# The low part of split weights made by a negated copy on ScalarE and an accumulating DMA, in place of a subtraction

## The chip, the cores and the metric

One core of a Trainium2 chip runs the whole kernel. The metric is the device time of one execution in microseconds (us). The kernel before was run three times: 1477.27, 1478.51 and 1480.23 us, so the median is 1478.51 us.

The engines are named as in the profile: PE is TensorE (matmuls), DVE is VectorE, ACT is ScalarE, POOL is GpSimd, SP is SyncE. SP does nothing here but issue DMAs; POOL and ACT issue some too.

## The reference, cut to what matters

Two layers of a sequence model over 512 tokens of 1024 features, batch 1, float32. Each layer has a projection of the normalised input, two kinds of mixers, an output projection, and a feed-forward part:

```
h = rms_norm(x, norm_mix[l]);  u = h @ w_in
layer 0: y = [hgrn2_mix(...), rwkv7_mix(...)] @ w_out
layer 1: y = [s5_mix(...), mlstm_mix(...)] @ w_out
x = x + y
h = rms_norm(x, norm_ffn[l])
x = x + (silu(h @ w_gate) * (h @ w_up)) @ w_down      # hidden size 2816
...
out = rms_norm(x, norm_final)
```

All that the change touches is how the weight matrices (`w_in`, `w_out`, `w_gate`, `w_up`, `w_down`) reach TensorE.

## The kernel before

Activations are kept transposed: features on the 128 partitions, the 512 tokens in the free dimension. A dense product is made of 128x128 blocks of weights against 128x512 blocks of activations. To keep float32 accuracy with the rounded type float32r, each operand is split into two parts, w = hi + lo and a = hh + hl, and every block takes three matmuls (`mm3`): hi with hh, hi with hl, lo with hh, in this order.

The weights are read from DRAM as **units**, listed in `order` in the order of their use. A full unit is 128x1024 (512 KB, eight blocks, 24 matmuls); the units of the output projections have 640 or 768 columns, and every third unit of a down projection (`wD`) has 768. `wget` hands out a unit and first calls `wissue` for the unit after it (AHEAD = 1). `wissue` does three things:

- SP loads the unit into one of two buffers `raw`.
- ACT copies it, 256 columns at a time, into float32r tiles `hi` (L369, in `split`). This rounds.
- DVE subtracts, lo = raw - hi, also 256 columns at a time (L370); for nine units of layer 0 (the list `pu`) POOL does it.

The pool `whl` has eight `hi` and eight `lo` tiles of 256 columns, which is two units of each. A tile is written again when the last matmul that reads its old content has ended, so the first quarter of a unit can be remade when a quarter of the unit two places before it has been used. Two narrow units (`wL`, `wG`) hold both parts side by side, and the last unit of the program is split into the tiles of the normalised input, which are free by then.

Each engine works through its own queue in order. The order in a queue is made when the program is built, by a scheduler that goes by the program's own order and by estimated costs; the names of tiles that it waits for are turned into semaphores.

Around this machinery the program has these stretches: layer 0's projections woven with the HGRN2 and RWKV-7 mixers (the RWKV-7 part inverts small triangular blocks on POOL, `rw_inverse`, and moves them by DMAs that POOL issues); the output projection (`wO0a`, `wO0b`); feed-forward part 0 (44 units `wGU0`, gate and up in turn, then 24 units `wD0`); layer 1's projections woven with S5 (POOL, with some twenty DMAs of its own) and mLSTM; the output projection (`wO1a`, `wO1b`); feed-forward part 1. In the feed-forward part (`ffn`) DVE takes a gate product out of PSUM (L1184), ACT applies Silu (L247), DVE multiplies the up product in (L1187, L1188), and ACT and DVE split the result into `ah` and `al`.

Of the kernel before, what the change touches and what calls it, by code (L numbers as in the profile page):

```python
# [11 lines left out]
F32R = mybir.dt.float32r  # L12
U32 = mybir.dt.uint32
AF = mybir.ActivationFunctionType
# [72 lines left out]
def _cols(w, cols):  # L87
    """[K, N] -> [len(cols)/128, 128, K]: per column tile, k tiles side by side."""
    a = w[:, cols]
    k, n = a.shape  # L90
    a = a.reshape(k // P, P, n // P, P)
    return np.ascontiguousarray(a.transpose(2, 1, 0, 3).reshape(n // P, P, k))


def _rows(w, cols, per):
    """[K, N] -> [K/(128 per), 128, per N]: per k tiles side by side, all columns."""
    a = w[:, cols]
    k, n = a.shape
    a = a.reshape(k // (P * per), per, P, n)
    return np.ascontiguousarray(a.transpose(0, 2, 1, 3).reshape(k // (P * per), P, per * n))  # L100


def _layout(i):
# [78 lines left out]
    # S5: partitions hold (group of the pair, state), free dims the pair of groups  # L182
# [20 lines left out]
def trunk(ctx: ExitStack, tc: tile.TileContext, A, out, dbg=None, start=0):  # L203
# [8 lines left out]
    class Pools:  # L212
        """pools that are opened one by one and closed together"""
# [25 lines left out]
    def act(o, i, f, bias=0.0, scale=1.0):  # L239
        """one table load for all the activations of a set that follow each other"""  # L240
        want = SETS.get(f)
        if want is not None and want != epoch["set"]:
            ld = S.preload_act_table_set(want)
            for u in epoch["users"]:
                tc.add_manual_dep(ld.ins, u, NOSYNC, reason="table")
            epoch.update(set=want, load=ld.ins.name, users=[])
        a = S.activation(o, i, f, bias=bias, scale=scale)  # L247
        if want is not None:
            tc.add_manual_dep(a.ins, epoch["load"], NOSYNC, reason="table")
            epoch["users"].append(a.ins.name)  # L250

    def sigmoid(o, x, nbias=0.0):
        """1 / (1 + exp(-x - bias)) by exp and ln alone"""
        act(o, x, AF.Exp, bias=nbias, scale=-1.0)
        act(o, o, AF.Ln, bias=1.0)
        act(o, o, AF.Exp, scale=-1.0)

    def newton(r_, v, t):
        """one step towards r_ = v ** -0.5"""
        act(t, r_, AF.Square)  # L260
        V.scalar_tensor_tensor(t, v, -0.5, t, MUL, MUL)  # L261
        V.scalar_tensor_tensor(r_, t, 1.5, r_, ADD, MUL)  # L262
# [14 lines left out]
    def ts(op, i, j, o, a, scale, bias, bias_s=None):  # L277
        """o = a * scale + bias"""
        e = on(op, i, j)
        if e is S:  # L280
            act(o, a, AF.Identity, bias=bias if bias_s is None else bias_s, scale=scale)
        else:
            e.tensor_scalar(o, a, scale, bias, MUL, ADD)
# [17 lines left out]
    # the weights in the order of their use, loaded and split ahead of it  # L301
# [20 lines left out]
    def onpool(unit, part):  # L322
        return unit in PRM["pu"] and part in PRM["c"]
# [7 lines left out]
    def wissue():  # L331
        nm, u, c0, n = order[pos[1]]
        raw = whl.tile([P, 1024], F32, tag="raw", name="raw", bufs=2)
        nc.sync.dma_start(raw[:, :n], A[nm][u][:, c0:c0 + n])
        parts = []
        last = nm == "wD1" and u == KD - 1
        if last and c0 == 0:
            wlast.extend(htiles()[:2])
        if nm in NARROW:
            # both parts of few columns, side by side  # L340
            m = NARROW[nm]
            for c in range(0, n, WP // 2):
                w = whl.tile([P, WP], F32R, tag=("hi", "lo")[len(parts) * m * 2 // WP % 2], name="w")
                w4 = w.rearrange("p (k s c) -> p k s c", s=2, c=m)
                split(w4[:, :, 0, :], w4[:, :, 1, :], raw[:, c:c + WP // 2].rearrange("p (k c) -> p k c", c=m))
                parts += [w[:, j:j + 2 * m] for j in range(0, WP, 2 * m)]
            n = 0
        for c in range(0, n, WP):
            m = min(n - c, WP)
            if last:  # L350
                hi, lo = (t.rearrange("p k t -> p (k t)")[:, c0 + c:c0 + c + m] for t in wlast)
            else:
                hi = whl.tile([P, WP], F32R, tag="hi", name="hi")
                lo = whl.tile([P, WP], F32R, tag="lo", name="lo")
            split(hi[:, :m], lo[:, :m], raw[:, c:c + m], G if onpool(pos[1], c // WP) else V)
            parts += [(hi[:, j:j + P], lo[:, j:j + P]) for j in range(0, m, P)]
        ready.append(parts)
        pos[1] += 1
# [8 lines left out]
    def split(h, l, src, eng=V):  # L367
        """src (SBUF, float32) = h + l"""
        S.copy(h, src)  # L369
        eng.tensor_tensor(l, src, h.bitcast(F32), SUB)  # L370
# [9 lines left out]
    def defer(f):  # L380
        """f after the next dense product; more banks until its result is there"""
        later.append(f)
        early[0] = PRM.get("d", 2)
# [27 lines left out]
    def run(gen, until=None):  # L411
        """advance a stream to its mark (or its end); its result"""
        while True:
            try:
                if next(gen) == until and until is not None:
                    return None
            except StopIteration as e:
                return e.value
# [4 lines left out]
    def weave(*streams):  # L423
        """emit streams side by side, each up to its mark, in proportion to the costs that they yield"""
        live = [[0.0, j, g, m] for j, (g, m) in enumerate(streams)]
        while live:
            e = min(live, key=lambda t: t[:2])
            v = next(e[2], None)
            if v is None or v == e[3]:
                live.remove(e)  # L430
            elif not isinstance(v, str):
                e[0] += v
# [5 lines left out]
    def beside(*gens):  # L438
        """streams side by side as one stream"""
# [10 lines left out]
    class Norm:  # L450
        """hh + hl = x * gain, tile by tile; rstd = 1 / rms of x on all partitions"""
# [72 lines left out]
    # ================= S5: discretised parameters, kept in DRAM until layer 1 =================  # L524
    def s5_setup(p5):
# [54 lines left out]
        # (lambda_bar - 1) / lambda  # L580
# [65 lines left out]
    # ================= layer 0: HGRN2 and RWKV-7 =================  # L646
    def layer0():
# [20 lines left out]
        # lower bounds: softmax over the table's rows, first row  # L668
# [14 lines left out]
        # 1 - ka, 1 - mu  # L683
# [27 lines left out]
        def hgrn(h):  # L711
# [30 lines left out]
            # attention inside the chunks: pairs of tokens, then blocks about their midpoints  # L742
# [9 lines left out]
            for l, n in enumerate((1, 32, 16, 8, 4, 2)):  # L752
                pp = mtile()
                if n > 1:
# [9 lines left out]
                    # only the columns of the later halves  # L764
# [12 lines left out]
            # states between the chunks  # L777
# [35 lines left out]
            # head norm, gain, gate  # L813
# [23 lines left out]
        # block-diagonal tiles: the zeros are written once  # L837
# [48 lines left out]
        def rw_prep(g, p):  # L886
# [7 lines left out]
            # decays up to a token (er) and up to the one before it (ea)  # L894
# [8 lines left out]
            # normalised key  # L903
# [18 lines left out]
            # bonus  # L922
# [4 lines left out]
            # products of the chunks  # L927
# [18 lines left out]
            # token-major forms  # L946
# [23 lines left out]
        def rw_inverse(q, g):  # L970
            """inverse of I - A on the diagonal blocks of 32 tokens, in place, a block per partition"""
# [48 lines left out]
        def rw_chain(g, p):  # L1020
            """states (values by keys) and outputs, chunk after chunk"""
# [25 lines left out]
            # norm over each head, bonus, gate  # L1047
# [128 lines left out]
    # ================= output projection, feed-forward =================  # L1176
    def ffn(l, x, hh, hl, rstd, pf, on_ready, side=()):
# [15 lines left out]
        for n in range(KD):  # L1193
            ps = dtile()
            if l == 1 and n == KD - 1:
                # half of the tokens after the other: the end of one beside the products of the next
# [67 lines left out]
    # ================= layer 1: S5 and mLSTM =================  # L1264
# [207 lines left out]
    AGI = {}  # L1472

    def gates():
# [6 lines left out]
        # log sigmoid  # L1481
# [12 lines left out]
        # sums over blocks of 128 tokens, running maximum  # L1494
# [25 lines left out]
        # rows of the heads to the partitions in ROW  # L1520
# [159 lines left out]
    # ================= final norm =================  # L1680
# [56 lines left out]
```

## Time and profile before

| | |
|---|---|
| median of three runs | 1478.51 us |
| span of the profiled execution | 1480.0 us |
| matmul records / weight loads | 6668 / 6668 |
| DVE, POOL subtractions of full tiles (128x256) at L370 | 759 x 462 ns, 34 x 882 ns |
| ACT casts 128x256 at L369 | 793 x 404 ns |
| DRAM traffic | 121.71 MB read, 10.39 MB written |

The page shows one execution on the chip. Busy times are per engine; a matmul's record is longer than its share of PE's time, since matmuls overlap in the array, so the rate is read from the starts of neighbouring matmuls. "PEclk" is the clock that TensorE was granted, 1.00 for full. In lists of waits, "A <- B" says that B ended A's wait.

### The profile page before, as it was taken

The numbers are of one execution on the slowest core, as the hardware profiler recorded it, in microseconds if no ns is written. First come the engines' busy times: TensorE is split into PE (matmuls) and PEld (weight loads), VectorE is DVE, ScalarE is ACT, GpSimd is POOL, SyncE is SP. The second block draws the span as 40 slices with busy tenths as digits, with TensorE's granted clock in tenths as the row PEclk, the third lists the DMA queues.
The fourth block names the chain that finished last, engine by engine and source line by source line (L and its number), as shares of the span: only waits on it lengthen the run. The fifth ranks groups of instructions, "written<-read, shape, count | busy, mean of one in ns | idle before, by whom it ended". The sixth has DMA issues, their size and how long they took to land. (4 is left out here: it accounts for less than half of the span.)

```text
span 1480.0 us, 19897 instructions
## 1 busy us (share of the span) xinstructions
PE 1423.6 (96%) x6668; PEld 1140.6 (77%) x6668; DVE 965.1 (65%) x2035; ACT 681.2 (46%) x1594; POOL 356.2 (24%) x538
## 2 busy tenths in 40 slices
PE   8989999988999999999999899999999999999996
PEld 5777878767787888888888678766778888888885
DVE  7589669899688555555444677679785555554333
ACT  7554565645465333333333333477464343333332
POOL 5367740678320333110010542100020000000001
PEclk9989989998999999999999999999999999999998
DMA  5211221021323333333343832311233323323331
GB/s 186 86 36 46 63 71 50 30 56 47 116 84 100 108 102 102 106 97 105 104 128 100 208 107 80 113 57 29 64 102 92 100 89 97 100 86 96 91 109 62
DMA packets 51142, 133.39 MB, mean 90 GB/s; under 512 B 10640, under 2 KB 16272, under 8 KB 50784
## 3 DMA queue, kind: packets, MB, share of 16 engines
q1 hardware_dynamic: 38656, 116.86, 25.9%
q0 software_dynamic: 3024, 7.26, 2.0%
q10 hardware_dynamic: 9360, 8.00, 1.8%
q8 instruction: 53, 0.87, 0.2%
q14 instruction: 49, 0.40, 0.1%
HBM read 121.71 MB, written 10.39 MB: 89 GB/s over the span
## 5 line engine op out<-in xcount | busy, mean ns | idle before, releaser
L369 ACT CAST hi<-raw 128x256 fp32r<-128x256 f32 (+1 forms) x809 | 317.9, 402 | 528.7 <-PE d L286 480.1
L370 DVE TENSOR_TENSOR lo<-raw,hi 128x256 fp32r<-128x256 f32 (+1 forms) x774 | 348.0, 459 | 295.3 <-ACT hi L369 281.1
L286 PE MATMUL d<-hh,hi 128*128 128x512 f32 x1088 | 443.3, 407 | 2.9 <-DVE ur L1077 2.9
L286 PE MATMUL d<-hl,hi 128*128 128x512 f32 x1088 | 438.9, 403 | 0.0
L286 PE MATMUL d<-hh,lo 128*128 128x512 f32 x1088 | 438.9, 403 | 0.0
L286 PEld LDWEIGHTS d<-hh,hi 128*128 128x128 f32 x1088 | 208.4, 192 | 52.7 <-DVE ur L1077 3.4
L286 PEld LDWEIGHTS d<-hh,lo 128*128 128x128 f32 x1088 | 208.2, 191 | 49.0 <-issue 1.1
L286 PEld LDWEIGHTS d<-hl,hi 128*128 128x128 f32 x1088 | 208.2, 191 | 48.7 <-issue 2.4
L286 PE MATMUL d<-ah,hi 128*128 128x512 f32 x330 | 129.4, 392 | 0.0
L286 PE MATMUL d<-ah,lo 128*128 128x512 f32 x330 | 129.4, 392 | 0.0
L286 PE MATMUL d<-al,hi 128*128 128x512 f32 x330 | 129.4, 392 | 0.0
L1706 POOL TENSOR_TENSOR x<-x,f 128x256 f32<-128x256 f32 x6 | 5.2, 890 | 368.7 <-issue 362.2
L286 PE MATMUL d<-ysp,hi 128*128 128x512 f32 x224 | 74.1, 407 | 2.6 <-DVE x L1164 0.9
L467 POOL TENSOR_TENSOR rstd<-rstd,sq 128x512 f32<-128x512 f32 x21 | 28.6, 1363 | 193.9 <-ACT sq L247 183.7
L980 POOL TENSOR_TENSOR iu<-iu,ti 32x30 f32<-32x30 f32 (+14 forms) x120 | 71.3, 594 | 9.2
L286 PEld LDWEIGHTS d<-ah,hi 128*128 128x128 f32 x330 | 61.9, 188 | 14.0
L286 PEld LDWEIGHTS d<-al,hi 128*128 128x128 f32 x330 | 61.9, 188 | 13.9
L286 PEld LDWEIGHTS d<-ah,lo 128*128 128x128 f32 x330 | 61.9, 188 | 13.8
L978 POOL TENSOR_TENSOR ti<-iu 32x30 f32<-32x30 f32 (+14 forms) x120 | 70.3, 586 | 9.0
L286 PEld LDWEIGHTS d<-ysp,hi 128*128 128x128 f32 x224 | 41.2, 189 | 12.9 <-issue 1.9
L1187 DVE TENSOR_TENSOR g<-d,g 128x512 f32<-128x512 f32 x42 | 29.0, 691 | 27.5 <-PE d L286 27.5
L286 PE MATMUL d<-ysp,lo 128*128 128x512 f32 x112 | 45.5, 406 | 0.7 <-DVE lo L370 0.7
(489 smaller groups left out, 2046.1 us busy)
## 6 DMA issues: line engine op xcount, KB each, us to landing
raw<-in_wGU_dram SPq DMA_DIRECT2D x88, 512.0 KB, 3.6
raw<-in_wD_dram SPq DMA_DIRECT2D x32, 512.0 KB, 3.6
raw<-in_wA_dram SPq DMA_DIRECT2D x16, 512.0 KB, 3.6
raw<-in_wB_dram SPq DMA_DIRECT2D x13, 512.0 KB, 3.7
raw<-in_wD_dram SPq DMA_DIRECT2D x16, 384.0 KB, 3.1
raw<-in_wV_dram SPq DMA_DIRECT2D x6, 512.0 KB, 5.3
raw<-in_wQ_dram SPq DMA_DIRECT2D x6, 512.0 KB, 3.7
raw<-in_wK_dram SPq DMA_DIRECT2D x6, 512.0 KB, 3.6
```

The lines of the kernel that those rows point to most:

```text
L286: T.matmul(o, w, a, start=start, stop=stop)
L369: S.copy(h, src)
L370: eng.tensor_tensor(l, src, h.bitcast(F32), SUB)
L467: self.eng.tensor_tensor(self.rstd, self.rstd, sq, ADD)
L978: G.tensor_tensor(t3, iu[:, j:j + 1, j + 1:].to_broadcast([32, j, n]), iu[:, 0:j, j:j + 1].to_broadcast([32, j, n]), MUL)
L980: G.tensor_tensor(iu[:, 0:j, j + 1:], iu[:, 0:j, j + 1:], t3, ADD)
L1187: V.tensor_tensor(g1, pu_, g1, MUL)
L1706: G.tensor_tensor(x[k][:, t], x[k][:, t], r_, MUL)
```

## The change

`wissue` is rewritten for all units but the first, the two narrow ones and the last of the program (three entries of `order`). For the 211 others:

- ACT makes `hi` in pieces of 512 columns, with four buffers (two units, as before).
- ACT also makes lo = -raw, rounded to float32r, in pieces of 512, into a tile `lo` of 1024 columns, with two buffers. Since rounding is symmetric, this is -hi.
- POOL then issues one DMA for the whole unit, which reads the weights from DRAM a second time and adds them to `lo` (`accum_op=ADD`). The sum is raw - hi.

The subtractions on DVE and POOL go. `raw` keeps its two buffers, SP's load is as before.

```
-        nc.sync.dma_start(raw[:, :n], A[nm][u][:, c0:c0 + n])
+        src = A[nm][u][:, c0:c0 + n]
+        nc.sync.dma_start(raw[:, :n], src)
...
-        for c in range(0, n, WP):
-            m = min(n - c, WP)
-            if last:
...
-            else:
-                hi = whl.tile([P, WP], F32R, tag="hi", name="hi")
-                lo = whl.tile([P, WP], F32R, tag="lo", name="lo")
-            split(hi[:, :m], lo[:, :m], raw[:, c:c + m], G if onpool(pos[1], c // WP) else V)
-            parts += [(hi[:, j:j + P], lo[:, j:j + P]) for j in range(0, m, P)]
...
+        else:
+            direct = pos[1] < PRM.get("direct", 1)
+            lo = whl.tile([P, 1024], F32R, tag="lo", name="lo", bufs=2)
+            for c in range(0, n, 512):
+                m = min(n - c, 512)
+                hi = whl.tile([P, 512], F32R, tag="hi", name="hi", bufs=4)
+                if direct:
+                    for e in range(0, m, 256):
+                        f = min(m, e + 256)
+                        split(hi[:, e:f], lo[:, c + e:c + f], raw[:, c + e:c + f])
+                else:
+                    S.copy(hi[:, :m], raw[:, c:c + m])
+                    S.activation(lo[:, c:c + m], raw[:, c:c + m], AF.Copy, scale=-1.0)
+                parts += [(hi[:, j:j + P], lo[:, c + j:c + j + P]) for j in range(0, m, P)]
+            if not direct:
+                G.dma_start(lo[:, :n], src, accum_op=ADD)
```

The rest of the diff takes comments out, so line numbers differ by 14 behind `wissue`: L286 stays, L369 and L370 of `split` become L383 and L384, and the new lines are L366 (hi), L367 (negated copy) and L370 (the DMA).

**ACT's queue in feed-forward part 0.** `hi_6708` and so on are 256-column pieces of one unit, `g1` is a gate tile on which Silu works, `ah18` a split result. Before:

```order
L369 CAST hi_6708<-raw_6706 128x256 [waits DMAHW6_49,PE_49,Activation_49]
L369 CAST hi_6712<-raw_6706 128x256 [waits PE_49,Activation_49]
L369 CAST hi_6716<-raw_6706 128x256 [waits PE_49,Activation_49]
L369 CAST hi_6720<-raw_6706 128x256 [waits PE_49,Activation_49]
L369 CAST hi_6754<-raw_6752 128x256 [waits DMAHW7_49,PE_49,Activation_49]
L369 CAST ah18_6687<-g1_6639 128x512 [waits DVE_49]
```

The same place now, for one gate unit (`lo_6154`) and the row behind it:

```order
L366 CAST hi_6155<-raw_6152 128x512 [waits DMAHW7_49,PE_49,Activation_49]
L366 CAST hi_6158<-raw_6152 128x512 [waits PE_49,Activation_49]
L367 ACTIVATE lo_6154<-raw_6152 128x512 [waits DMASW6_49,PE_49,Activation_49]
L247 ACTIVATE g1_6149<-g1_6149 128x512 [waits DVE_49]
L367 ACTIVATE lo_6154<-raw_6152 128x512
L366 CAST hi_6210<-raw_6207 128x512 [waits DMAHW0_49,PE_49,Activation_49]
```

Each quarter of `hi` waited for PE on its own; now the first half of `lo` waits for PE once for its whole buffer, and a Silu stands between the two halves in every second unit.

**PE's queue at a unit's start in the same part.** `d` is the PSUM tile, `hh` and `hl` the two parts of the activations. Before, two blocks of a unit (the third row has no wait, since DVE's subtraction is covered by the wait ahead of it):

```order
L286 MATMUL d_6770<-hh_4449,hi_6708 128x512 [waits DVE_49,Activation_49]
L286 MATMUL d_6770<-hl_4450,hi_6708 128x512
L286 MATMUL d_6770<-hh_4449,lo_6709 128x512
L286 MATMUL d_6770<-hh_4449,hi_6708 128x512
L286 MATMUL d_6770<-hl_4450,hi_6708 128x512
L286 MATMUL d_6770<-hh_4449,lo_6709 128x512
```

Now:

```order
L286 MATMUL d_6124<-hh_4181,hi_6061 128x512 [waits DVE_49,Activation_49]
L286 MATMUL d_6124<-hl_4182,hi_6061 128x512
L286 MATMUL d_6124<-hh_4181,lo_6060 128x512 [waits DMASW6_49,Activation_49]
L286 MATMUL d_6124<-hh_4181,hi_6061 128x512
L286 MATMUL d_6124<-hl_4182,hi_6061 128x512
L286 MATMUL d_6124<-hh_4181,lo_6060 128x512
```

The third matmul of every unit now waits for a DMA issued by POOL (`DMASW`), and that DMA covers all eight blocks.

**POOL's queue in layer 1, at the end of S5.** `scr_y` and `ys` are transfers of S5's output through DRAM, `lo` the accumulating DMAs of the projections beside it. Now:

```order
L1455 DMA scr_y<-yg 16x16x64
L370 DMA lo<-in_wS_dram 128x1024
L1455 DMA scr_y<-yg 16x16x64 x7
L370 DMA lo<-in_wS_dram 128x1024 x2
L1459 DMA ys_8145<-scr_y 128x512
L1459 DMA ys_8194<-scr_y 128x512
L370 DMA lo<-in_wQ_dram 128x1024
L1651 MEMSET dt 128x512
```

Before, the rows of `scr_y` and `ys` stood there without the rows of L370 between them: POOL's queue held no part of the weights in layer 1.

More of the change, by code (lines that the diff above doesn't have):

```diff
@@ L341, in wissue @@
             m = NARROW[nm]
-            for c in range(0, n, WP // 2):
-                w = whl.tile([P, WP], F32R, tag=("hi", "lo")[len(parts) * m * 2 // WP % 2], name="w")
+            for c in range(0, n, 256):
+                w = whl.tile([P, 512], F32R, tag="hi", name="w", bufs=4)
                 w4 = w.rearrange("p (k s c) -> p k s c", s=2, c=m)
-                split(w4[:, :, 0, :], w4[:, :, 1, :], raw[:, c:c + WP // 2].rearrange("p (k c) -> p k c", c=m))
-                parts += [w[:, j:j + 2 * m] for j in range(0, WP, 2 * m)]
@@ L347, in wissue @@
-            n = 0
-        for c in range(0, n, WP):
-            m = min(n - c, WP)
-            if last:
-                hi, lo = (t.rearrange("p k t -> p (k t)")[:, c0 + c:c0 + c + m] for t in wlast)
-            else:
-                hi = whl.tile([P, WP], F32R, tag="hi", name="hi")
-                lo = whl.tile([P, WP], F32R, tag="lo", name="lo")
-            split(hi[:, :m], lo[:, :m], raw[:, c:c + m], G if onpool(pos[1], c // WP) else V)
-            parts += [(hi[:, j:j + P], lo[:, j:j + P]) for j in range(0, m, P)]
+                split(w4[:, :, 0, :], w4[:, :, 1, :], raw[:, c:c + 256].rearrange("p (k c) -> p k c", c=m))
@@ new lines, in wissue @@
+                parts += [w[:, j:j + 2 * m] for j in range(0, 512, 2 * m)]
+        elif last:
+            for c in range(0, n, 256):
+                m = min(n - c, 256)
+                hi, lo = (t.rearrange("p k t -> p (k t)")[:, c0 + c:c0 + c + m] for t in wlast)
+                split(hi, lo, raw[:, c:c + m])
+                parts += [(hi[:, j:j + P], lo[:, j:j + P]) for j in range(0, m, P)]
+        else:
[14 more added lines that the diff above has]
+                G.dma_start(lo[:, :n], src, accum_op=ADD)
```

## The prediction

> **What bounds the kernel now.** The page's first part is read first.
>
> ```profile
> span 1480.0 us, 19897 instructions
> ...
> PE 1423.6 (96%) x6668; PEld 1140.6 (77%) x6668; DVE 965.1 (65%) x2035; ACT 681.2 (46%) x1594; POOL 356.2 (24%) x538
> ```
>
> TensorE is busy for 96%: at most 56 us can be won without less matmul work, and the change leaves the matmuls alone. Next, the stretches of the program, since an average hides where DVE matters. The columns behind the stretch are its length, then busy time of PE, PEld, DVE, ACT and POOL, the clock, the DMA share and GB/s.
>
> ```profile
> 8.00:63.00 55.00, 54.84 (x224) 40.48 (x223) 33.72 (x65) 38.65 (x88) 21.54 (x27) 1.00 0.39 130
> 63.00:450.00 387.00, 361.06 (x2002) 296.96 (x2001) 320.40 (x683) 209.06 (x530) 205.85 (x336) 0.94 0.21 63
> 450.00:678.00 228.00, 228.00 (x999) 183.63 (x998) 138.66 (x327) 89.83 (x208) 46.85 (x74) 1.00 0.33 102
> 678.00:800.00 122.00, 122.00 (x538) 100.67 (x537) 55.35 (x110) 47.04 (x108) 6.50 (x5) 1.00 0.36 108
> 1081.00:1326.00 245.00, 243.67 (x1040) 195.42 (x1039) 139.36 (x273) 104.11 (x234) 9.54 (x7) 1.00 0.31 95
> 1326.00:1466.00 140.00, 140.00 (x665) 115.72 (x664) 55.90 (x121) 46.67 (x110) 2.73 (x3) 1.00 0.30 89
> ```
>
> The last four rows are the feed-forward parts, about half of the span: PE has no gap there, and DVE is busy for 40 to 61%. Taking subtractions from DVE can win nothing there. Only in 63 to 450 us is DVE near full (320 of 387) while PE idles, for 387 - 361 = 26 us. That is the most that the relief of DVE can give.
>
> **How much time a unit has.** The order of instructions shows that PE's third matmul of a unit will wait for the accumulating DMA. So the question is when that DMA can land. Neighbouring rows in a feed-forward part:
>
> ```profile
> 563.34 0.40 PE L286 MATMUL d<-hh,hi 128*128 128x512 f32 x1
> ...
> 563.58 0.39 PE L286 MATMUL d<-hl,hi 128*128 128x512 f32 x1
> ...
> 563.81 0.40 PE L286 MATMUL d<-hh,lo 128*128 128x512 f32 x1
> ...
> 564.06 0.41 ACT L369 CAST hi<-raw 128x256 fp32r<-128x256 f32 x1 [0.99 <-PE d L286]
> ```
>
> Matmuls start 0.233 us apart, though each record is 0.39 long. A full unit of 24 takes 5.6 us, one of 768 columns (18) 4.2. A buffer comes free when the last matmul that reads it ends, 0.39 - 0.23 = 0.16 after its slot; ACT starts 0.09 later (563.58 + 0.39 = 563.97, then 564.06). Before, that hand-over ran quarter by quarter with a whole unit of lead. Now `lo` has two buffers, each a whole unit: the buffer for unit u is free at the end of unit u-2, and must be refilled, DMA included, while unit u-1 runs. PE needs it two matmuls (0.47) into unit u. So the refill is free only within 5.6 + 0.47 = 6.07 us.
>
> **The refill, c, term by term.** Its ACT part, from the nearest rows:
>
> ```profile
> L247 ACT ACTIVATE g<-g 128x512 f32<-128x512 f32 x44 | 27.8, 632 | 23.5 <-DVE g L1184 23.5
> L369 ACT CAST ah<-g 128x512 fp32r<-128x512 f32 x44 | 27.3, 620 | 12.6 <-DVE g L1188 11.4
> L247 ACT ACTIVATE hh<-x,par 128x512 fp32r<-128x512 f32 x32 | 23.1, 721 | 17.9 <-DVE x L1673 7.1 <-DVE x L1226 5.5 <-DVE x L1209 4.3
> ```
>
> After the buffer is free ACT does the second `hi` (its buffer is freed by the same end), the first `lo`, in every gate unit a Silu, and the second `lo`: 0.62 + 0.62 + 0.63 + 0.62 = 2.49 us, or 1.86 without the Silu. A negated copy is taken at the cast's 0.62; the row with a scale, 0.72, is the other bound and would add 0.2. With 0.25 for the release and 0.1 each for POOL to see ACT and for PE to see the DMA, c = 2.94 + X in the gate units and 2.31 + X elsewhere, where X is the DMA from issue to landing. No accumulating DMA is in this trace. Its neighbours:
>
> ```profile
> raw<-in_wGU_dram SPq DMA_DIRECT2D x88, 512.0 KB, 3.6
> raw<-in_wD_dram SPq DMA_DIRECT2D x16, 384.0 KB, 3.1
> wt<-scr_wt POOLq DMA_DIRECT2D x1, 1024.0 KB, 7.9
> yraw<-scr_yb SPq DMA_DIRECT2D x2, 256.0 KB, 2.7
> ys<-scr_y POOLq DMA_DIRECT2D x2, 256.0 KB, 3.2
> raw<-in_wG_dram SPq DMA_DIRECT2D x1, 256.0 KB, 2.6
> ```
>
> A plain 512 KB issued by POOL is 3.6 + (3.2 - 2.7) = 4.1. Lower bound: X = 4.1, the second operand free. The second operand has to be read, too; 256 KB more cost 3.6 - 2.6 = 1.0, so 512 KB cost 2.0. And SP's load of a later unit waits for the same second `lo` (it frees `raw`), so both transfers start together on the same 16 engines: between 0 and another 2.0. Upper bound from these rows 8.1, close to POOL's 1 MB beside other loads (7.9). I take X = 4.1 + 2.0 + 0.75 = 6.85, because SP's load starts 0.5 earlier and about 1.5 us of it are shared half and half. For 768 columns: 3.1 + 0.5 + 1.5 + 0.75 = 5.85.
>
> The Trainium skill, "DMA: Bandwidth & Descriptors", section "Anatomy of one DMA — SWDGE (gpsimd) path", gives a GpSimd-issued DMA 2.0 us plus its bytes at 436 GB/s, which would be 3.2 us here, and c = 6.1. By it the refill hides, and the time stays near 1480. The trace disagrees already for plain loads, with 3.6 from SP's queue.
>
> **Two buffers, so two units per round.** Unit u ends no earlier than the landing plus its remaining 22 matmuls (5.13), and the next turn of this buffer starts there: two units take c + 5.13 instead of 11.2.
>
> PE's gap then is c - 6.07 = 3.7 us in each pair of gate and up. Such a gap costs more than itself:
>
> ```profile
> 135.90 0.79 PE L286 MATMUL d<-hh,hi 128*128 128x512 f32 x1 [2.70 <-DVE ur L1077]
> ...
> 136.91 0.63 PE L286 MATMUL d<-hh,lo 128*128 128x512 f32 x1
> 137.34 0.63 PE L286 MATMUL d<-hh,hi 128*128 128x512 f32 x1
> ...
> 394.56 1.16 PE L286 MATMUL r<-pb,wu 128*128 128x128 f32 x8 [1.37 <-DVE wu L275]
> ...
> 840.10 1.12 PE L1344 MATMUL m<-con,vf 128*128 128x128 f32 x4 [4.19 <-DVE vf L1340]
> ...
> 841.45 0.63 PE L286 MATMUL d<-hh,hi 128*128 128x512 f32 x1
> 841.87 0.63 PE L286 MATMUL d<-hl,hi 128*128 128x512 f32 x1
> ...
> 838.70:845.50 6.80, 5.40 (x15) 4.45 (x16) 5.79 (x12) 2.68 (x6) 6.33 (x11) 0.51 1.00 172
> ```
>
> After gaps of 2.70 and 4.19 us matmuls start 0.43 apart, at a granted clock of about 0.5; the second time nine of them, so 9 x (0.43 - 0.233) = 1.7 us are lost. I add h = 1.7 to each round with a gap over 2 us.
>
> The Trainium skill, "TensorE: Matmul & The Clock Gate", section "Part 1: The HAM clock gate", has the clock fall after an idle window of about 3.4 us. By it the gaps below of 3.1 us in `wD` would keep the clock (38 us less). The trace has it fall after 2.70, so the row decides.
>
> **The sum**, against the profile's 1480.0 (the median of the runs is 1.5 lower).
>
> - Gate and up, 88 units, 44 pairs: c = 2.94 + 6.85 = 9.79; 9.79 + 5.13 + 1.7 = 16.6 for 11.2: +5.4 a pair, **+238**.
> - `wD`, 15 column tiles of 1024, 1024, 768: c = 9.16 twice, and 0.25 + 1.42 + 0.2 + 5.85 = 7.7 (ACT: 0.40 + 0.62 + 0.40); with d - 0.47 of 5.13, 5.13, 3.73 the half sum is 20.0 for 15.4, so 4.6, and 1.7 x 3/2 = 2.5 for the clock: 7.1 x 15, **+107**.
> - 8 units of `wO0b`, `wO1b`: (7.7 + 3.73 + 1.7 - 8.4)/2 = 2.4 each, **+19**.
> - The first ten units, dense in 8 to 63 us: (9.16 + 5.13 + 1.7 - 11.2)/2 = 2.4 each, **+24**.
> - Units woven with mixers:
>
> ```profile
> 195.13 34.59 SPq L334 DMA_DIRECT2D raw<-in_wA_dram  x4
> ...
> 815.38 34.72 SPq L334 DMA_DIRECT2D raw<-in_wV_dram  x6
> ...
> 1002.28 58.24 SPq L334 DMA_DIRECT2D raw<-in_wO1a_dram  x8
> ```
>
> Loads are issued there 7 to 12 us apart, and a unit needs (9.16 + 5.13)/2 = 7.1: mostly covered by the other matmuls, **+10**; if it isn't, some 30.
> - POOL's queue. The DMAs stand between steps of `rw_inverse` and of S5 and wait for ACT, and those behind wait with them; and a `lo` of `wQ` stands behind S5's second `ys`:
>
> ```profile
> POOL ys L1445 <- DVE yc L1448: 22.7, 1, 22.7
> ```
>
> That row bounds the stall by 0 and 23; **+15**.
> - DVE's relief in 63 to 450 us: 0 to 26, **-15**. ACT's extra there, 2.48 for 1.62 a unit, lies in its idle half.
> - DVE's and POOL's subtractions elsewhere, SP's loads and the DRAM traffic (a third of the engines' time): 0, hidden as before. If the engines filled up, X would grow, which the upper bound holds.
>
> Sum: 238 + 107 + 19 + 24 + 10 + 15 - 15 = **+398**, so 1878 by the profile; I forecast 1877.
>
> **Rivals.**
> 1. *The refill hides, and DVE's relief is left: faster.* Decides at X = 3.1 (c = 6.07). For it: the skill's formula, and POOL's 256 KB in 3.2. Against: every 512 KB row is 3.6 or more. It gives 1480 - 26 = 1454 at best, 1480 if POOL's queue takes it back. Chance 4%.
> 2. *The second operand is free, and loads don't collide*, X = 4.1. Gate and up: a gap of 0.97 a pair, under the 1.37 that left the clock alone, 43 us; `wD`: c = 6.41 twice and 5.47, (18.3 + 14.0)/2 - 15.4 = 0.75 x 15 = 11; the rest 5 to 15. Time 1540 to 1550. For it: DMA engines are busy for a third in the dense stretches. Against: twice the bytes are read. Up to X = 5.5, where half the gaps halve the clock and the time is some 1680. Chance 20%.
> 3. *Accumulating is slower than all neighbours, or collides fully*, X of 8.1 and more. Gate and up: 11.04 + 5.13 + 1.7 - 11.2 = 6.7 x 44 = 293; `wD` 132; others 52 and up to 55 for woven units and POOL's queue: about 2010. For it: POOL's 1 MB took 7.9 beside other loads. Chance 26%, half of it over 2130.
> 4. *The change doesn't do what it says* (a scheduler that puts PE's `lo` matmuls later): the queue printed above excludes it.
>
> **Chances.** The forecast, X of 5.5 to 8.1, has 50%. The range leaves out rival 1 and half of rival 3: 1540 to 2130. Differences under 0.2% (3 us) can't be told from no change here. Faster 3%, same 1%, slower 96%.
>
> **What would show it.** PE gaps in the feed-forward parts at a unit's third matmul, ended by the DMA of `lo`, one in two units; the landing time of `lo<-in_wGU_dram` near 6.9; a clock that falls to 0.5 again and again; two units in 16.6 us instead of 11.2; DVE's busy time down by about 330 us with nothing won by it. The prediction is wrong if landings are under 4 or over 9 us, or if gaps lie with ACT or POOL's queue instead.

## The result, and the profile after

| | before | after |
|---|---|---|
| median | 1477.89 us (4 runs, 1476.17 to 1480.23) | 1980.22 us (4 runs, 1976.98 to 1985.90) |
| ratio | | 1.3395, 95% interval 1.3365 to 1.3424 |
| profiled span | 1480.0 us | 1980.8 us |

The kernel is a third slower, by 502 us. The prediction was 1877, with a range of 1540 to 2130.

From the page of the changed kernel: the span and busy times, the granted clock over 40 slices, the queue of POOL's DMAs (packets, MB, share of the DMA engines), then costly groups (busy time, mean, idle time just before), and last the DMA issues with their median time from issue to landing.

```profile
span 1980.8 us, 19127 instructions
...
PE 1580.9 (80%) x6668; PEld 1225.0 (62%) x6668; DVE 651.1 (33%) x1262; ACT 828.5 (42%) x1630; POOL 494.7 (25%) x714
...
PEclk8898988888898988999898888899889999889988
...
q0 software_dynamic: 33408, 111.74, 31.5%
...
L286 PE MATMUL d<-hh,lo 128*128 128x512 f32 x1088 | 478.2, 440 | 219.2 <-DMA lo<-in_wGU_dram 150.4
...
L286 PE MATMUL d<-ah,lo 128*128 128x512 f32 x330 | 141.2, 428 | 70.8 <-DMA lo<-in_wD_dram 64.2
...
raw<-in_wGU_dram SPq DMA_DIRECT2D x88, 512.0 KB, 4.3
lo<-in_wGU_dram POOLq DMA_DIRECT2D x88, 512.0 KB, 7.4
...
lo<-in_wD_dram POOLq DMA_DIRECT2D x30, 512.0 KB, 6.5
```

Three things are to be read off. DVE is busy for 314 us less (965.1 before), and nothing came of it. PE is idle for 1980.8 - 1580.9 = 400 us, where it was 56, and 219.2 + 70.8 = 290 of them stand before the matmuls that read `lo`. And PE's busy time itself grew by 157 us with the same 6668 matmuls: that is the clock, at 0.8 in more than half of the slices.

PE's list of waits gives the releaser of each:

```profile
PE d L286 <- DMA lo<-in_wGU_dram: 150.4, 43, 4.7
PE d L286 <- DMA lo<-in_wD_dram: 64.2, 25, 5.5
PE d L286 <- DMA lo<-in_wA_dram: 26.7, 9, 8.3
PE d L286 <- DMA lo<-in_wB_dram: 19.0, 6, 4.7
```

88 gate and up units have 43 waits, so one in two units, 150.4 / 43 = 3.5 us each. One of them in the time line (start, length, engine, line, operation; in brackets the idle time before and what ended it):

```profile
1706.09 0.62 ACT L366 CAST hi<-raw 128x512 fp32r<-128x512 f32 x1 [3.16 <-PE d L286]
...
1706.61 0.63 ACT L367 ACTIVATE lo<-raw 128x512 fp32r<-128x512 f32 x1
...
1707.15 0.61 ACT L247 ACTIVATE g<-g 128x512 f32<-128x512 f32 x1
...
1707.67 0.61 ACT L367 ACTIVATE lo<-raw 128x512 fp32r<-128x512 f32 x1
...
1708.31 5.41 SPq L335 DMA_DIRECT2D raw<-in_wGU_dram  x2
...
1708.57 0.86 POOL L370 DMA_DIRECT2D lo<-in_wGU_dram  x1 [11.11 <-ACT lo L367]
...
1716.73 0.77 PE L286 MATMUL d<-hh,lo 128*128 128x512 f32 x1 [4.44 <-DMA lo<-in_wGU_dram]
...
1717.30 0.63 PE L286 MATMUL d<-hh,hi 128*128 128x512 f32 x1
```

This is the refill in the order that the prediction gave it: ACT's `hi`, `lo`, Silu and `lo` from 1706.09 to 1708.28 (2.19 us, since each starts about 0.52 behind the one before; the prediction added whole durations, 2.49), POOL's DMA at 1708.57, SP's load 0.26 us ahead of it, and PE's third matmul at 1716.73, 8.2 us after the issue. The next matmul starts 0.57 later and lasts 0.63 instead of 0.39.

The stretches of the program, cut where SP issues the first load of the next part. Lengths in us, worked out from these issues:

| kernel | start to `wGU0` | gate/up 0 | `wD0` | `wC` to `wO1a` (mixers of layer 1) | `wO1a`, `wO1b` | gate/up 1 | `wD1` to end |
|---|---|---|---|---|---|---|---|
| before | 424.6 | 253.3 | 121.6 | 202.8 | 79.0 | 244.3 | 154.4 |
| after | 513.0 | 366.5 | 172.9 | 261.6 | 95.6 | 367.9 | 203.2 |
| difference | +88.4 | +113.2 | +51.3 | +58.8 | +16.6 | +123.6 | +48.8 |
| e1, no DMA | 428.6 | 249.7 | 122.2 | 199.2 | 76.0 | 243.8 | 153.4 |
| e4, three buffers in feed-forward | 505.7 | 280.5 | 122.2 | 256.1 | 94.1 | 254.5 | 154.4 |
| e5, DMA in feed-forward alone | 422.3 | 365.9 | 178.3 | 209.6 | 82.0 | 365.3 | 206.2 |
| e6, DMA elsewhere alone | 512.5 | 259.0 | 123.4 | 251.5 | 93.3 | 250.0 | 151.3 |
| e9, half-unit buffers | 468.1 | 285.7 | 123.5 | 223.5 | 85.0 | 246.2 | 154.0 |
| e11, e9 with POOL's queue cleared | 462.9 | 255.7 | 121.8 | 217.4 | 85.7 | 247.4 | 155.2 |
| e12, e1 with POOL's queue cleared | 453.8 | 250.5 | 122.2 | 197.1 | 76.0 | 243.8 | 150.9 |

Gate and up lost 113.2 + 123.6 = 237 us, `wD` 100: the prediction had 238 and 107. The other three stretches lost 164, where it had 24 + 19 + 10 + 15 - 15 = 53. That is where its 103 us are missing (111, less the 8 by which gate, up and `wD` were put too high). The experiments first settle what costs, then look into this term.

### The profile page after: what moved, and what is told of

It is laid out like the page before. It is cut to its first block, busy times and chain, and to the rows that moved or that the text cites. A ratio compares the mean times of both kernels' runs of the same rounds, so it can differ in the third digit from the quotient of the medians.

```text
span 1980.8 us, 19127 instructions
## 1 busy us (share of the span) xinstructions
PE 1580.9 (80%) x6668; PEld 1225.0 (62%) x6668; DVE 651.1 (33%) x1262; ACT 828.5 (42%) x1630; POOL 494.7 (25%) x714
## 5 line engine op out<-in xcount | busy, mean ns | idle before, releaser
L286 PE MATMUL d<-hh,lo 128*128 128x512 f32 x1088 | 478.2, 440 | 219.2 <-DMA lo<-in_wGU_dram 150.4
L366 ACT CAST hi<-raw 128x512 fp32r<-128x512 f32 (+2 forms) x422 | 250.8, 594 | 877.3 <-PE d L286 657.2
L286 PE MATMUL d<-hh,hi 128*128 128x512 f32 x1088 | 475.4, 437 | 1.9 <-DVE vf L1354 1.0
L286 PE MATMUL d<-hl,hi 128*128 128x512 f32 x1088 | 468.6, 431 | 0.0
L286 PEld LDWEIGHTS d<-hh,lo 128*128 128x128 f32 x1088 | 227.7, 209 | 303.3 <-issue 189.0
L286 PEld LDWEIGHTS d<-hl,hi 128*128 128x128 f32 x1088 | 227.8, 209 | 57.6 <-issue 3.4
L286 PEld LDWEIGHTS d<-hh,hi 128*128 128x128 f32 x1088 | 228.2, 210 | 56.8 <-issue 4.3
L367 ACT ACTIVATE lo<-raw 128x512 fp32r<-128x512 f32 (+2 forms) x422 | 242.0, 596 | 5.0 <-PE d L286 1.8
L370 POOL DMA_DIRECT2D lo<-in_wGU_dram x88 | 76.1, 865 | 572.2 <-ACT lo L367 520.3
L286 PE MATMUL d<-ah,lo 128*128 128x512 f32 x330 | 141.2, 428 | 70.8 <-DMA lo<-in_wD_dram 64.2
L286 PE MATMUL d<-ah,hi 128*128 128x512 f32 x330 | 137.8, 418 | 0.0
L286 PE MATMUL d<-al,hi 128*128 128x512 f32 x330 | 137.6, 417 | 0.0
L1198 DVE TENSOR_TENSOR g<-d,rstd 128x512 f32<-128x512 f32 x42 | 29.1, 692 | 318.1 <-PE d L286 318.1
L286 PEld LDWEIGHTS d<-ah,lo 128*128 128x128 f32 x330 | 67.6, 205 | 98.4 <-issue 49.6
L370 POOL DMA_DIRECT2D lo<-in_wD_dram x45 | 38.9, 865 | 260.9 <-ACT lo L367 238.9
L286 PE MATMUL d<-ysp,hi 128*128 128x512 f32 x224 | 80.4, 434 | 1.6 <-DVE x L1178 1.6
L286 PEld LDWEIGHTS d<-al,hi 128*128 128x128 f32 x330 | 67.0, 203 | 16.1
L286 PEld LDWEIGHTS d<-ah,hi 128*128 128x128 f32 x330 | 67.4, 204 | 14.5
L286 PE MATMUL d<-ysp,lo 128*128 128x512 f32 x112 | 49.5, 443 | 27.2 <-DMA lo<-in_wO0a_dram 15.5
```

What stands on the lines that cost most here:

```text
L286: T.matmul(o, w, a, start=start, stop=stop)
L366: S.copy(hi[:, :m], raw[:, c:c + m])
L367: S.activation(lo[:, c:c + m], raw[:, c:c + m], AF.Copy, scale=-1.0)
L370: G.dma_start(lo[:, :n], src, accum_op=ADD)
L1198: V.tensor_tensor(g1, pg, rstd, MUL)
```

## Experiments: what of the change costs

Each is an edit of the changed kernel. e3 and e9 ran four times, every other one once; seven runs of the kernel before lay between 1474 and 1481 us, so a few us in a total mean nothing.

**e1: without the DMA.**

```
-            if not direct:
-                G.dma_start(lo[:, :n], src, accum_op=ADD)
```

> The changed kernel without its accumulating DMAs (the second part of the weights stays at the negated first part). Theory A (the landing of the DMA closes a refill of c = 2.9 us + 7.4 us that fits into 6.07 us only without the DMA): refill 2.7 us, PE gaps at the third matmul of a unit gone, 1455 to 1485 us. Rival B (the copies that ScalarE now makes in 512-column pieces, and the order of its queue, cost much of the 502 us): 1550 us or more.

Measured: 1474.81 us, 1478.03 before. The whole loss is the DMA. The rest of the change (ACT's copies, the larger buffers, the new order, the relief of DVE and POOL) comes out 3 us faster as a net, which is within the spread of the kernel before, and the start of the program, where the relief was to win 15 us, is 4 us longer (428.6 for 424.6). A variant that keeps these copies and adds a DMA can hardly be much below 1475.

**e2: the same DMA without the addition.**

```
-                G.dma_start(lo[:, :n], src, accum_op=ADD)
+                G.dma_start(lo[:, :n], src)
```

> The same DMAs without the add (the second part of the weights becomes the unsplit weights). If reading the second operand costs what the prediction said (2.0 us of the landing): landing of 512 KB in the gate and up units 5.4 us instead of 7.4, a pair of units in 2.94 + 5.4 + 5.13 = 13.5 plus up to 1.7 us instead of 16.6, time 1700 to 1830 us. If adding costs nothing and the path from GpSimd with the collision is slow as such: landing 7 us or more, time 1950 us or more.

Measured: 1676.1 us, below what was expected; the landing was 4.6, not 5.4.

**e7: the addition from `raw`, which lies in SBUF already.** SP's next load into this `raw` then waits for the DMA, but the load into the other `raw` still runs beside it, begun earlier.

```
+                G.dma_start(lo[:, :n], raw[:, :n], accum_op=ADD)
```

> The accumulating DMA reads the weights from the buffer raw in SBUF instead of a second time from DRAM, so SP's next load must wait for it and can't run beside it. If the collision with that load costs 0.75 us of the landing, as the prediction said, landing 6.6 us in gate and up and 0.8 us less a pair plus less clock loss: 1900 to 1950 us. If the collision costs the whole 2 us: landing 5.4 us, 1800 us. If it costs nothing: 1980 us.

Measured: 1733.22 us, below all three numbers. The landing rows, first of e2, then of e7:

```profile
lo<-in_wGU_dram POOLq DMA_DIRECT2D x88, 512.0 KB, 4.6
```

```profile
lo<-raw POOLq DMA_DIRECT2D x172, 512.0 KB, 5.1
```

In the gate and up units no run has the adding DMA with nothing beside it. In e7 a load starts about 1.2 us ahead of it there:

```profile
1411.85 0.33 SPq L335 DMA_DIRECT2D raw<-in_wGU_dram  x1
1413.05 0.86 POOL L370 DMA_DIRECT2D lo<-raw  x1 [6.77 <-ACT lo L367]
```

Among the mixers, though, the changed kernel and e7 have adding DMAs that run alone. While the changed kernel's DMA that is issued at 154.56 is under way no other is issued, and the same holds for e7's at 107.22. Their landings:

```profile
lo<-in_wB_dram POOLq DMA_DIRECT2D x1, 512.0 KB, 5.8
```

```profile
lo<-raw POOLq DMA_DIRECT2D x1, 512.0 KB, 4.6
```

(Three more of the changed kernel with little beside them, at 231.28, 350.37 and 365.71, took 5.7 to 5.9.) So the second operand costs 5.8 - 4.1 = 1.7, where the prediction had 2.0 (the 4.1 of a plain DMA is its estimate), and the meeting with SP's load 7.4 - 5.8 = 1.6, where it had 0.75. A plain DMA loses, by the same estimate, only 4.6 - 4.1 = 0.5 to the load. From SBUF the addition takes 4.6 instead of 5.8, so e7 gained by its source as well as by the later meeting.

The time of a pair of gate and up units, from SP's issues, checks the formula of the round, c + 5.13: e2 2.94 + 4.6 + 5.13 = 12.7, measured 12.5; e7 2.94 + 5.1 + 5.13 = 13.2, measured 13.0. The 2.19 us of ACT instead of 2.49 are about this difference. (e7 proves less, since ACT there waits for `raw` too, 3.68 us at 1409.46.) In both the gaps in gate/up 1 are at most 2.0 us, but for a single one (4.0 us in e2, 2.6 in e7), and the granted clock of gate/up 1 was 0.99 (it stands behind the busy times in this row of e7; behind it are DMA share and GB/s):

```profile
1276.40:1561.60 285.20, 255.66 (x1044) 193.84 (x1044) 64.53 (x94) 130.73 (x228) 42.72 (x48) 0.99 0.68 162
```

In the changed kernel it was 0.89. So e7 lost nearly the whole fall of the clock as well, of which its expectation had counted only a part.

**e8: 14 matmuls into a spare PSUM tile in each gate unit's gap.**

```
+                mm(ps, w[k][0], hh[:, k, :], k == 0, False)
+                mm(ps, w[k][0], hl[:, k, :], False, False)
+                if fill and k == 0:
+                    pf_ = mtile()
+                    for j in range(fill):
+                        mm(pf_, w[0][0], hh[:, 0, :], j == 0, j == fill - 1)
+                mm(ps, w[k][1], hh[:, k, :], False, k == KD - 1)
```

> After's kernel with 14 matmuls more in each gate unit of the feed-forward parts, between its second and third matmul, into a spare PSUM tile that nobody reads; 14 x 0.233 = 3.3 us, which lie in the gap of 4.4 us. What the half clock costs by itself: if the fall of the clock after a gap costs some 1.7 us a pair as predicted, 44 x 1.7 = 75 us less, about 1905; 1900 to 1930. If the slow matmuls after a gap cost nothing (they'd only lie in time in which the next refill is awaited), 1980 or more, since the round is set by the refill alone.

Measured: 1958.24 us, between the two cases. The windows of gate/up 1 (length; busy time of PE, PEld, DVE, ACT, POOL; clock, DMA share, GB/s), first of the changed kernel, then with the filler:

```profile
1409.70:1777.60 367.90, 283.15 (x1045) 218.65 (x1044) 67.07 (x97) 134.36 (x235) 46.79 (x51) 0.89 0.60 125
```

```profile
1407.10:1751.30 344.20, 319.06 (x1339) 250.34 (x1338) 67.17 (x97) 134.88 (x235) 46.87 (x51) 1.00 0.61 134
```

294 matmul records more, and 23.7 us less: work put into a gap shortens the stretch, since the clock stays at 1.00. Gate/up 0 lost 366.5 - 354.2 = 12.3, so 36 us in 44 pairs, 0.8 each; landings were 0.3 longer here (7.7 for 7.4), which makes it about 1.1. The prediction had 1.7. PE's busy time in gate/up 1 had grown by some 39 us, from the 243.67 of the row for 1081 to 1326 us to 283.15, which is 1.8 a pair; why only a part of it comes back was not settled. The stretch of the mixers of layer 1, in which nothing was edited, came out 12 us longer in this run, which is why the total shows only 22.

**e3: the eight `lo` matmuls of a unit at its end** (in projections and `wD`; wO units as before).

```
-                mm3(ps, *w[k], hh[:, k, :], hl[:, k, :], k == 0, k == KD - 1)
+                mm(ps, w[k][0], hh[:, k, :], k == 0, False)
+                mm(ps, w[k][0], hl[:, k, :], False, False)
...
+            for k in range(KD):
+                mm(ps, w[k][1], hh[:, k, :], False, k == KD - 1)
```

> In each dense unit of 1024 or 768 columns of the projections and feed-forward parts, all products of the first weight part come first and the eight of the second part last, so PE asks for the DMA 16 matmuls (3.7 us) into the unit. Theory A: two units take c + 8 x 0.233 = 10.3 + 1.9 = 12.2 us instead of 16.6, the down projections hide; gate and up win 44 x 4.4 = 190, down 90 us, woven units part of their loss: 1620 to 1720 us. Rival C (the DMA engines or DRAM are the limit, a landing just comes later when more is asked for): over 1850 us.

Measured: 1619.67 us (ratio to before 1.0949, 1.0921 to 1.0977), just at the lower bound of what was expected. With the same DMAs, landing at 7.7, the place of the wait alone recovers 360 of 502 us.

**e4: three `lo` buffers in the feed-forward parts, `lo` made ahead of `hi`.**

```
+                lo = deep[0].tile([P, 1024], F32R, tag="lo3", name="lo", bufs=3)
...
+                    if wide and c == 0:
+                        S.activation(lo[:, :512], raw[:, :512], AF.Copy, scale=-1.0)
+                        S.activation(lo[:, 512:n], raw[:, 512:n], AF.Copy, scale=-1.0)
...
+                if wide and c == 0:
+                    G.dma_start(lo[:, :n], src, accum_op=ADD)
```

> Three lo buffers instead of two in the feed-forward units, and ACT makes both lo copies, and POOL issues the DMA, ahead of the hi copies. Theory A (latency: a buffer is refilled only after its last use, and two buffers leave one unit of time for it): three units may then take c + 5.13 = about 15.5 us against 3 x 5.6 = 16.8 of matmuls, so the refill hides, the 337 us of the feed-forward parts vanish, and the time is 1630 to 1680. Theory B (throughput: the accumulating DMA can't keep up, one 512 KB in 5.6 us beside the load): landings get longer, and the time stays over 1850.

Measured: 1669.17 us, as theory A has it. It is latency against two buffers, not bandwidth: the same bytes are moved in 254.5 us of gate/up 1 instead of 367.9. (The third buffer and the earlier issue were not tried apart.) SP's load now starts 1.3 or 1.8 us ahead of the adding DMA instead of 0.27, and the landing is 5.8 instead of 7.4. One thing was not expected: gate/up 0 still took 280.5. e11 bears on it.

## Experiments: the units outside the feed-forward parts

**e5 and e6: the DMA in the feed-forward units alone, and in the others alone.**

```
-            direct = pos[1] < PRM.get("direct", 1)
+            direct = nm[:2] not in ("wG", "wD")
```

> The accumulating DMA is kept for wGU and wD alone; all other units (mixers, output projections, first ten) get their second part by DVE's subtraction from the same two raw and lo buffers. Theory A (the stretches lose apart from each other: after's feed-forward stretches are 337 us longer than before's, the others 164): only the 337 stay, 1478 + 337 = about 1815 us, 1795 to 1835, and the stretches outside are within 15 us of before's. Theory B (the woven stretches lose because the new buffers and ACT's copies are later there, not because of the DMA): they stay long, and the time is over 1900.

```
+            direct = pos[1] < 1 or nm[:2] in ("wG", "wD")
```

> The reverse: the accumulating DMA for all units but wGU and wD, whose second part DVE makes. Theory A (woven stretches lose 164 us by themselves): 1478 + 164 = about 1640 us, 1620 to 1660, with PE's gaps there ended by DMA lo. By the sum of my prediction (10 + 15 - 15 + 19 + 24 = 53 for these units): 1530. Theory B (their loss comes from feed-forward units, by POOL's queue or loads that are late at the borders): under 1560.

Measured: 1831.33 and 1642.72 us, with 1476.74 before: +354.6 and +166.0. That is 521 together for 502 in one kernel: the two losses stand side by side, and the second is three times the 53 of the prediction. Theory A holds in both.

**e10: the DMA in the first ten units and in `wO0b`, `wO1b` alone.**

```
+            direct = not (0 < pos[1] < 11 or nm in ("wO0b", "wO1b"))
```

> The accumulating DMA only where my prediction costed units outside the feed-forward parts one by one: the first ten units and wO0b, wO1b; DVE's subtraction everywhere else. By those two terms, 24 + 19, 1478 + 43 = 1521, 1505 to 1540; then the rest of the 165 us that the units outside the feed-forward parts lose, some 120, lies with the units woven with mixers and with POOL's queue, which the prediction gave 10 + 15 - 15. If instead it was the dense terms that were too small, 1580 or more.

Measured: 1519.49 us, 1478.68 before: +41 for the predicted 24 + 19 = 43 (by SP's issues, 28 of it up to `wGU0` and 5 in the `wO1` units; the rest is scattered over stretches that have no such DMA). So the other units, woven with mixers, and POOL's queue cost 166 - 41 = 125 us, where the prediction had 10 + 15 - 15 = 10.

Why, is seen in SP's issues. Units of layer 1 that the prediction called woven, before:

```profile
865.08 0.33 SPq L334 DMA_DIRECT2D raw<-in_wQ_dram  x1
892.40 0.33 SPq L334 DMA_DIRECT2D raw<-in_wK_dram  x1
...
935.87 0.33 SPq L334 DMA_DIRECT2D raw<-in_wK_dram  x1
941.47 0.33 SPq L334 DMA_DIRECT2D raw<-in_wQ_dram  x1
947.07 0.33 SPq L334 DMA_DIRECT2D raw<-in_wK_dram  x1
952.67 0.33 SPq L334 DMA_DIRECT2D raw<-in_wQ_dram  x1
```

And units of the same two matrices after:

```profile
1155.71 0.33 SPq L335 DMA_DIRECT2D raw<-in_wQ_dram  x1
1166.24 0.33 SPq L335 DMA_DIRECT2D raw<-in_wK_dram  x1
1172.96 0.33 SPq L335 DMA_DIRECT2D raw<-in_wQ_dram  x1
1183.73 0.33 SPq L335 DMA_DIRECT2D raw<-in_wK_dram  x1
1189.54 29.16 SPq L335 DMA_DIRECT2D raw<-in_wS_dram  x3
```

Before, the last four loads are 5.6 us apart, exactly a unit's matmuls: there is no mixer work between them. After, two units take 17.2 and 16.6 us, as in the gate and up parts. "7 to 12 us apart" was the mean of a stretch in which dense runs of 5.6 alternate with pauses (27.3 in the first two rows), and a pause does not help the dense run behind it. PE at this place:

```profile
1157.33 0.47 PE L286 MATMUL d<-hh,lo 128*128 128x512 f32 x1 [2.71 <-DMA lo<-in_wV_dram]
...
1174.64 0.48 PE L286 MATMUL d<-hh,lo 128*128 128x512 f32 x1 [3.38 <-DMA lo<-in_wK_dram]
```

In the whole stretch of layer 1's mixers, PE's waits for accumulating DMAs are 25.8 us, and its busy time grew from 195.3 to 215.2 us at a clock of 0.88 for 0.96. That is 46 of the 58.8 us lost there. The prediction's term for these units had no price for the clock.

**e9: buffers of half a unit, four of them, with a DMA each.** No more memory than the changed kernel takes.

```
-            lo = whl.tile([P, 1024], F32R, tag="lo", name="lo", bufs=2)
...
+                lo = whl.tile([P, 512], F32R, tag="lo", name="lo", bufs=4)
...
+                    S.activation(lo[:, :m], raw[:, c:c + m], AF.Copy, scale=-1.0)
+                    G.dma_start(lo[:, :m], src[:, c:c + m], accum_op=ADD)
+                    S.copy(hi[:, :m], raw[:, c:c + m])
```

> The same memory, cut finer: four lo buffers of half a unit instead of two of a whole one, each with its own accumulating DMA of 256 KB, and ACT makes the half's lo copy ahead of its hi copy. Theory A (what costs is latency against one unit of time: a buffer is refilled only while the one other buffer is used): a half is free for three halves, 3 x 2.8 + 0.47 = 8.9 us, and its refill takes 0.25 + 0.62 + 0.2 + X; X lies between POOL's plain 256 KB (3.2) and the 7.4 of the whole unit, so at most 8.5, and it hides in the feed-forward parts and in the woven ones alike: 1475 to 1520, what is left of it in the stretches where POOL's queue holds the DMAs. Theory B (the transfers themselves are the limit: after's DMA share in the gate and up parts is 0.63 at 16.6 us a pair, which is 0.93 at 11.2): landings grow past 9 us, and the time stays over 1600.

Measured: 1582.78 us (ratio 1.0697, 1.0678 to 1.0717), so 397 of 502 us are back, yet 63 more are left than theory A allowed. Gate/up 1, `wD0` and `wD1` are as without the DMA, within 3 us (table): latency is the cause there. DMAs of 256 KB landed after 5.6, and the DMA engines carried it at the very share that theory B feared:

```profile
1185.80:1432.10 246.30, 244.60 (x1044) 196.00 (x1045) 68.41 (x97) 134.51 (x236) 86.47 (x96) 1.00 0.93 188
```

The start (+39.5 over e1), gate/up 0 (+36.0) and the mixers of layer 1 (+24.3) are what is left. In the start, POOL's time line shows the reason; L991 and L993 are the steps of `rw_inverse`, L995 and L1004 its transfers through DRAM, L367 the accumulating DMAs:

```profile
199.93 0.25 POOL L991 TENSOR_TENSOR ti<-iu 32x30 f32<-32x30 f32 x1
200.26 0.33 POOL L993 TENSOR_TENSOR iu<-iu,ti 32x30 f32<-32x30 f32 x1
200.89 0.55 POOL L995 DMA_DIRECT2D scr_u<-iu  x1 [0.30 <-POOL iu L993]
204.13 1.68 POOL L1004 DMA_DIRECT2D ub<-scr_u  x3 [2.69 <-DMA scr_u<-iu]
205.80 0.97 POOL L367 DMA_DIRECT2D lo<-in_wA_dram  x1
```

```profile
200.42 0.62 ACT L366 ACTIVATE lo<-raw 128x512 fp32r<-128x512 f32 x1
```

```profile
209.70 0.79 PE L286 MATMUL d<-hh,lo 128*128 128x512 f32 x1 [9.15 <-DMA lo<-in_wA_dram]
```

ACT's negated copy is done at 201.04, but the DMA is issued at 205.80, behind the round trip of `scr_u`, and PE waits for 9.15 us. POOL's queue accounts for 4.8 of these.

**e11 and e12: POOL's queue cleared of most of the mixers' work,** with the DMA (e9's form) and without it (e1's). Some memsets and products stay. Beside the edits shown, the entry 'dq' of the table PRM, which names the queues of `rw_inverse`'s DMAs, goes from 'aggg' to 'asss'.

```
-    ENG = {"V": V, "S": S, "G": G}
+    ENG = {"V": V, "S": S, "G": V}
-                cmul(G, o[:, 0], o[:, 1], pwr[:, q, 0:n].unsqueeze(3).to_broadcast(shp),
+                cmul(V, o[:, 0], o[:, 1], pwr[:, q, 0:n].unsqueeze(3).to_broadcast(shp),
-                G.tensor_tensor(t3, iu[:, j:j + 1, j + 1:].to_broadcast([32, j, n]),
+                V.tensor_tensor(t3, iu[:, j:j + 1, j + 1:].to_broadcast([32, j, n]),
...
-            nc.gpsimd.dma_start(d, s)
+            nc.sync.dma_start(d, s)
```

> The kernel with half-unit buffers, with POOL's queue cleared of the mixers' work: rw_inverse's 60 steps, S5's complex products and every step that the table gives to G run on VectorE, and their DMAs on SP's queue, so that POOL issues little but the accumulating DMAs. That kernel stands 108 us over the one without any DMA (1582.8 and 1474.8); the same moves are made in the one without DMA in the run beside this one, since they have a price of their own. Theory A (the rest is the wait of the DMAs in POOL's queue behind such steps, as in PE's wait of 9.15 us at 209.70): this kernel stands at most 40 us over its partner, with the 30 us of the first gate and up part gone. Theory B (it is bandwidth, or matmuls in a fixed order behind a DMA that is late by itself): still 80 to 110 over.

> The same moves from POOL to VectorE and SP in the kernel without the accumulating DMA (the second part is then the negated first part alone): the partner of the run beside it. VectorE takes over some 150 us in the first 430 us, where it was busy for 290, and small steps there are shorter than POOL's: 1460 to 1520 us.

Measured: 1547.81 and 1496.03 us. The difference is 51.8, against 108 before the clearing: between the two theories, nearer to A. By the table, the start stands 462.9 - 453.8 = 9 us over its partner (39.5 without clearing) and gate/up 0 5 us (36.0; there S5's complex products on POOL had stood ahead of the DMAs, in e4 too). But the mixers of layer 1 still stand 20 us over (24.3), and the wO1 units 9.7 (9.0). The windows of these mixers, e11 first and e12 behind it, show a DMA share of 0.76 for 0.41, more idle time of PE (17 for 6 us), and 9 us more of busy time at a lower clock:

```profile
840.40:1057.80 217.40, 200.01 (x901) 154.44 (x900) 112.03 (x213) 112.75 (x203) 52.30 (x64) 0.94 0.76 167
```

```profile
826.40:1023.60 197.20, 190.97 (x900) 148.77 (x899) 110.05 (x213) 111.47 (x201) 6.73 (x12) 0.97 0.41 113
```

Of the idle time in e11, 8.4 us are waits for accumulating DMAs of `wC` and `wV`. The longest of them shows that POOL's queue still has a part:

```profile
856.26 0.62 ACT L366 ACTIVATE lo<-raw 128x512 fp32r<-128x512 f32 x1
```

```profile
858.42 2.24 POOL L1301 MEMSET kb<- 64x512 f32 x4
860.89 0.88 POOL L367 DMA_DIRECT2D lo<-in_wC_dram  x1 [0.22 <-PE m L286]
```

```profile
870.26 0.80 PE L286 MATMUL m<-hh,lo 128*128 128x512 f32 x1 [5.20 <-DMA lo<-in_wC_dram]
```

The copy is done at 856.88, but the DMA stands behind memsets until 860.89, and its 256 KB land only after 9.3 us, beside a load and transfers of S5. So theory A is not excluded here, and a meeting of transfers takes part too; how the 30 us of layer 1 divide stays open.

No version here beats the kernel before: with the DMA in all units e11 is the best, and e1 shows no gain beyond the spread of the runs.

## Why the prediction was right in most, and where it was not

- **The mechanism was right**: two buffers of a whole unit, refilled through ACT, POOL and DMA within one unit's time, a gap at the third matmul of every second unit, and the clock falling behind it. e1 (the DMA is all of it), e3 (it is where the wait stands) and e4 (the number of buffers, with an earlier issue) show it. The time lies inside the range, 103 us over the forecast.
- **Gate and up, +238, measured +237.** The pair took 16.55 us for 16.6, and that is closer than its terms deserve. X is 7.4, not 6.85, since the meeting with SP's load was put too low (0.75 for 1.6) and the second operand a little too high (2.0 for 1.7). Against it, the clock costs some 1.1 a pair, not 1.7, and ACT 0.3 less: 2.64 + 7.4 + 5.13 + 1.1 = 16.3, so 0.3 is not accounted for.
- **`wD`, +107, measured +100; the dense units outside, +43, measured +41.** Both totals stand. In `wD0` waits cost 39 us and the clock 12, where the prediction had 34.5 and 19, so errors cancel there too.
- **DVE's relief, -15: none is seen** in e1, whose start is 4 us longer.
- **The mis-sized term is that of the woven units and of POOL's queue**: 10 + 15, or +10 with the relief, measured about 125. The step that failed is "Loads are issued there 7 to 12 us apart, and a unit needs (9.16 + 5.13)/2 = 7.1: mostly covered by the other matmuls". It took a mean over a stretch for the time of each unit. In the dense runs between the pauses the full price of a gate pair is paid (17.2 and 16.6 us for two units), with the fall of the clock, which this term left out. How the 125 divides was measured only on e9's form: the finer buffers took 94 of the 164 us away from these stretches, the dense units' 41 among them at most, and 70 were left. Of these, some 30 in the start are POOL's queue (e11 and e12), some 30 in layer 1 were explained only in part. The 15 for POOL's queue was sized by a row of S5's `ys` alone; a wait of 9.15 us behind `rw_inverse` was not in it. In gate/up 0 the changed kernel shows nothing of that queue, its 366.5 being no more than the 367.9 of gate/up 1: there the wait for the DMA seems to cover it.
- **Rivals.** That the refill hides, or that X is 4.1, is excluded by the landing of 7.4. That accumulating is slower than all neighbours gave nearly the right time, 2010, but by the wrong terms: its X of 8.1 was not met, and it put 293 us on gate and up, where 237 were measured.
- **The Trainium skill.** The estimate of 3.2 us for such a DMA by the formula of the Trainium skill, "DMA: Bandwidth & Descriptors" ("Anatomy of one DMA — SWDGE (gpsimd) path"), was not met here: the plain one took 4.6 beside a load, the adding one 5.8 alone and 7.4 beside a load. The Trainium skill, "TensorE: Matmul & The Clock Gate" ("Part 1: The HAM clock gate"), has the clock fall after an idle window of about 3.4 us. Behind the gap of 2.71 us shown above (1157.33) matmuls are 0.43 apart from 1158.91 on, so here too the clock fell after less:

```profile
1159.34 0.63 PE L286 MATMUL d<-hh,hi 128*128 128x512 f32 x1
1159.77 0.63 PE L286 MATMUL d<-hl,hi 128*128 128x512 f32 x1
```

## What to carry to other kernels

A producer with a long latency needs buffers by latency, not by bytes: ask how long a buffer has between its last use and its next one, and cut the same memory into smaller pieces (two whole units cost 502 us here, four halves 104) or put the consumer's wait later (some 140 us). Look at this unit by unit: a mean spacing over a stretch hides the dense runs, and pauses elsewhere don't pay for them. A DMA that an engine issues waits in that engine's queue behind its arithmetic and behind its other DMAs' waits, so count those steps too.

## What was not expected of the hardware

- 512 KB that are added from DRAM to a tile land after 5.8 us alone and after 7.4 when another 512 KB load starts 0.27 us ahead, though the engines' mean share was only 0.60 in gate/up 1. With the load 1.3 or 1.8 us ahead (e4) the landing is back at 5.8. When the adding DMA had half the size (e9), the engines ran at a share of 0.93 and 188 GB/s with PE at full speed. So a mean share of 0.6 says little about two transfers that start together.
- Idle matmul time can be cheaper when filled: useless matmuls in the gaps of gate/up 1 (294 records more) made it 23.7 us shorter.
